# A decoder layer on one core: a shared scratch pool, parameters spread over the dense products, two scan sets ahead of the attention's end, paired sample values, later feed-forward row scales and four result buffers

## The chip, the core and the metric

The kernel runs on 1 core of a Trainium2 chip. TensorE (PE in the profile) multiplies matrices, VectorE (DVE), ScalarE (ACT) and GpSimd (POOL) do the elementwise work, and SyncE (SP) mostly issues transfers. The metric is the device time of one execution in microseconds (us).

## The reference

One layer of a hybrid decoder serves a prompt of 1024 tokens and 8 sample sequences of 4 tokens, 1056 tokens in all, of width 1024, in float32. Each sublayer normalizes its input and adds its result to the stream x:

```
proj = rms_norm(x) @ w_in                         # u (512), q, k, v (512 each)
ssm  = s5(u)            # per channel group: Bu, diagonal complex scan over time, C h + D u, GLU
o    = diff_attention(q, k, v)                    # 4 heads, two softmax maps each, causal
x    = x + concat(ssm, o) @ w_out
x    = x + cross_attention(rms_norm(x), memory)   # 4 heads, 256 memory tokens, ca_wq, ca_wo
h    = rms_norm(x)
x    = x + (silu(conv3(h @ ffn_wg)) * (h @ ffn_wv)) @ ffn_wd   # hidden width 2816
```

The samples attend to 512 cached positions (a paged cache, gathered by a page table) and to cached memory keys and values of their own. The scan starts from zero for the prompt and from a given state for the samples. Keys, values, scan states, the last convolution rows and the memory's keys and values are results too.

## The kernel before, in words

**Products.** A float32 product is done as three products of split operands: `split` (L165) makes a high part on ScalarE and the low rest on VectorE, and `mm3` (L186 to L189) multiplies high by high (L187), high by low (L188) and low by high (L189). Activations lie transposed, channels on partitions and tokens along the free axis, in `Xh` and `Xl`; weights come in blocks of 128 columns as `raw` and are split into `whi` and `wlo`. Tokens are cut into nine tiles (`TILES`: eight of 128 and one of 32) and three column blocks (`TB`: 384, 384 and 288). VectorE and ScalarE calls go through a wrapper, so that all of them carry the line L56; tiles tell them apart.

**Order of the work.** The first part of the layer is written as generators that issue a piece of work and yield a cost estimate. `par` and `drive` (L78, L104) always advance the generator whose sum of costs, divided by a given total, is lowest; a third number in a stream's entry is the share at which it starts, and `until` holds a stream until a name stands in `done`. So the totals `R`, the offsets `S` and the yields set the order in which instructions are written, and with it their place in each engine's queue. The call of `drive` (L1499) runs ten streams: the dense products (`dense_all`, L850), the scan's parameters (`params`), the prompt's attention (`attention_all`), the opening of pools, the scan's table loads, scan sets and outputs (`ssm_tables`, `ssm_datas`, `ssm_outs`, L1090 to L1115), the memory's keys and values, the samples' attention and the samples' scan state.

**Parameters.** `ssm_params` (L330 to L445) computes the discretized scan parameters in scratch that a small allocator (`Carve`, L194) cuts out of four tiles named `scr`. These lie in the tags qT, kT, vt and s3 of the pool `hdB` (L457, L491), which head 1's projections use later, so `dense_all` holds head 1 until `params` is done (L852). Its eight steps yield 100 each. `ssm_setup` (L936 to L992) then builds four tables per quarter in the pool `tb` (L456), among them products `kp` (L967), and stores them to DRAM.

**Heads.** `dense_head` projects q, k and v of one head; `attention` (L680 to L738) computes scores in the two buffers of `ps_s` (tag S), turns the softmax weights `P` and multiplies by values. `open_right` (L900) opens pools when all dense products are done, and `open_left` (L910) opens others when the attention is closed, adding 'left' to `done`.

**Scan sets.** The 512 scan channels are handled in four sets. `ssm_data(q)` (L1009 to L1047) loads the set's inputs `Ug` by SP's queue, waits for 'left', multiplies them into `wp` (L1021), rotates the result by VectorE (`va`, `vb`, `vr`, `vi`), runs eight scans of 128 steps and rotates back into `Hr` and `Hi`. `ssm_out(q)` (L1049) multiplies the states out and turns the result `yt` back (`tp_`, L1087).

**Output gate and w_out.** In the pool block `p4`, `gate(d, b, ...)` (L1569) does one 128-row block of the GLU gate (`zp`) for column block b. At b == 1, `turn_samples` (L1355) transposes the second half of the samples' attention result (`os_` into `po`, L1356), and the mixed rows go to DRAM, from where `load_part` (L1540) loads them for column block b. `update_x` (L1512) adds a product to x and adds its squares to `sqa` (on GpSimd, L1527); `token_rstd` (L1529) sums `sqa` over channels (`sp`, L1534) and computes the tokens' scales `r2`.

**Cross-attention.** The samples' values are 16 groups of four products (`Op`, L1893) in `sample_values` (L1878 to L1917), each with a tile `vt` of 512 KB that GpSimd's queue loads (L1884) into three buffers. They run beside the output projection `ca_wo` (`wo_stage`, L1921), whose parts for the last column block wait for them. `token_rstd` is called at the end (L1955).

**Feed-forward.** `R3`, the scales broadcast over partitions, is made by nine products and nine VectorE copies (L1974 to L1979). For each of 22 hidden blocks `up(m)` (L2001) does three gate blocks (`pg`), scales them by `R3`, does three value blocks (`pv`), then convolution and silu; after each pair of hidden blocks `down` (L2061) multiplies by `ffn_wd` and adds to `xacc`. `xacc` itself is filled from `Xh + Xl` (L2091). Behind the last pair the results are transposed (`pt`, L2078), copied by ScalarE into `yo` (two buffers) and stored row tile by row tile (L2071 to L2082).

**Stages in the trace.** Dense products and attention of the heads run from the start to about 475 us (dense products to about 372), gates from about 550 to 607, w_out to 717, cross-attention to 912, ca_wo to 1026, the feed-forward from there to 1811, the last results to 1822 us.

## Time and profile before

| | |
|---|---|
| median of 3 runs | 1820.39 us (1814.05 to 1829.77) |
| profiled execution | 1823.91 us, span 1822.0 us |
| TensorE busy | 1713.6 us, 94% of the span |
| VectorE, ScalarE, GpSimd busy | 1088.7, 602.8, 509.3 us |
| mean granted clock of TensorE | 0.961 of full speed |

The profile is of one execution; its span runs from the first to the last instruction, and the execution's own time is 1.9 us longer. Busy time of an engine is the time in which one of its instructions ran. PEld is TensorE's loading of weights, which overlaps its products; a name with a q behind it is the engine's sequencer. In a line of the timeline, `out<-in` are the tiles by the program's names, `128x512` partitions by elements, `xN` the number of instructions run together in the line, and what stands in brackets is the idle time of the engine just before it and what ended it. The granted clock is the share of TensorE's full speed that the chip allowed.

### The profile page before, as it was taken

The page shows a single profiled execution, that of the slowest core. Times are in us where ns is not written, and L with a number is a line of the kernel's source. Part 1 is how long each engine was busy: PE and PEld are TensorE (multiplying, and loading weights), DVE is VectorE, ACT ScalarE, POOL GpSimd, SP SyncE. Part 2 cuts the span into 40 slices and gives each one's busy share as a digit, 9 for nine tenths or more (in the row PEclk, how much of TensorE's full clock was granted, in tenths as well). Part 3 has the DMA queues.
Part 4 walks back from the last instruction along what each step waited for, and adds up shares of the span by engine and source line. Part 5 has one row for each costly group of instructions (what it writes and reads, how often), then busy time and mean ns, then how long its engine had stood idle before and what let it go on. Part 6 is the DMA issues. An engine that isn't in the chain of part 4 may idle for free.

```text
span 1822.0 us, 28691 instructions
## 1 busy us (share of the span) xinstructions
PE 1713.6 (94%) x11121; PEld 1596.7 (88%) x11121; DVE 1088.7 (60%) x2563; ACT 602.8 (33%) x1368; POOL 509.3 (28%) x597
## 2 busy tenths in 40 slices
PE   8679999989797899999899999999999999999998
PEld 7458788767685899999769999999999999999997
DVE  6867635666587586555546654654654565555653
ACT  6535335566355343444433211210210211111112
POOL 4456675130300043000033332322312312322210
PEclk9878999989898999999989999999999999999999
DMA  6512232155785722323272111210211211202202
GB/s 174 217 49 80 89 87 91 40 178 172 213 270 163 263 59 64 102 91 94 84 239 70 39 40 31 70 43 28 58 48 35 58 37 46 59 25 58 58 13 97
DMA packets 151809, 170.02 MB, mean 93 GB/s; under 512 B 9528, under 2 KB 125396, under 8 KB 151675
## 3 DMA queue, kind: packets, MB, share of 16 engines
q1 hardware_dynamic: 129650, 114.04, 20.6%
q0 software_dynamic: 10944, 31.95, 5.8%
q10 hardware_dynamic: 11080, 22.21, 3.3%
q8 instruction: 87, 1.43, 0.3%
q14 instruction: 48, 0.39, 0.1%
HBM read 131.86 MB, written 36.30 MB: 92 GB/s over the span
## 4 chain that ended last, share of the span: by engine, by line
PE 79%; DVE 8%; ACT 4%; DMA 3%; issue 1%; SPq 1%; ACTq 0%; POOL 0%; DVEq 0%; POOLq 0%
PE pp L187 5%; PE pp L188 5%; PE pp L189 5%; PE pv L189 5%; PE pv L187 5%; PE pv L188 5%; PE pd L189 5%; PE pd L188 5%; PE pd L187 5%; PE pg L187 5%; PE pg L188 5%; PE pg L189 4%; PE pj L187 2%; PE S L694 2%; PE pj L189 2%; PE pj L188 2%
## 5 line engine op out<-in xcount | busy, mean ns | idle before, releaser
L56 DVE TENSOR_TENSOR xacc<-xacc,pd 128x384 f32<-128x384 f32 (+1 forms) x264 | 135.1, 518 | 169.9 <-PE pd L189 169.9
L56 ACT CAST whi<-raw 128x1024 fp32r<-128x1024 f32 x74 | 77.4, 1049 | 434.0 <-PE pg L188 332.1
L187 PE MATMUL pv<-Xh,whi 128*128 128x384 f32 (+1 forms) x528 | 172.0, 326 | 0.0
L189 PE MATMUL pv<-Xh,wlo 128*128 128x384 f32 (+1 forms) x528 | 171.7, 326 | 0.0
L188 PE MATMUL pv<-Xl,whi 128*128 128x384 f32 (+1 forms) x528 | 171.6, 325 | 0.0
L187 PE MATMUL pd<-ah,dhi 128*128 128x384 f32 (+1 forms) x528 | 171.2, 325 | 0.1
L187 PE MATMUL pg<-Xh,whi 128*128 128x384 f32 (+1 forms) x528 | 171.2, 324 | 0.0
L189 PE MATMUL pd<-ah,dlo 128*128 128x384 f32 (+1 forms) x528 | 170.9, 324 | 0.0
L188 PE MATMUL pd<-al,dhi 128*128 128x384 f32 (+1 forms) x528 | 170.1, 322 | 0.5 <-DVE al L56 0.5
L188 PE MATMUL pg<-Xl,whi 128*128 128x384 f32 (+1 forms) x528 | 170.6, 323 | 0.0
L189 PE MATMUL pg<-Xh,wlo 128*128 128x384 f32 (+1 forms) x528 | 170.1, 322 | 0.0
L56 DVE TENSOR_TENSOR wlo<-raw,whi 128x1024 fp32r<-128x1024 f32 x74 | 108.8, 1471 | 27.7 <-ACT whi L56 21.5
L799 POOL TENSOR_TENSOR raw<-raw,GT 128x1024 f32<-128x1024 f32 x30 | 69.3, 2311 | 158.8 <-DMA raw<-in_ffn_wg_dram 99.4
L187 PE MATMUL pp<-Mh,whi 128*128 128x384 f32 (+1 forms) x336 | 108.9, 329 | 2.5 <-ACT Mh L56 2.5
L187 PE MATMUL pj<-whi,Xh 128*128 128x384 f32 (+1 forms) x288 | 103.0, 360 | 8.0 <-DVE vt L56 7.5
L188 PE MATMUL pp<-Ml,whi 128*128 128x384 f32 (+1 forms) x336 | 109.6, 328 | 0.0
L189 PE MATMUL pp<-Mh,wlo 128*128 128x384 f32 (+1 forms) x336 | 109.5, 327 | 0.0
L188 PE MATMUL pj<-wlo,Xh 128*128 128x384 f32 (+1 forms) x288 | 100.5, 350 | 6.3 <-DVE wlo L56 6.3
L189 PE MATMUL pj<-whi,Xl 128*128 128x384 f32 (+1 forms) x288 | 100.8, 350 | 0.0
L189 PEld LDWEIGHTS pv<-Xh,wlo 128*128 128x128 f32 x528 | 100.0, 189 | 0.1
L187 PEld LDWEIGHTS pv<-Xh,whi 128*128 128x128 f32 x528 | 100.0, 189 | 0.0
L188 PEld LDWEIGHTS pd<-al,dhi 128*128 128x128 f32 x528 | 99.2, 188 | 0.8 <-DVE al L56 0.8
(788 smaller groups left out, 4508.8 us busy)
## 6 DMA issues: line engine op xcount, KB each, us to landing
raw<-in_ffn_wg_dram SPq DMA_DIRECT2D x22, 512.0 KB, 3.9
raw<-in_ffn_wv_dram SPq DMA_DIRECT2D x22, 512.0 KB, 3.9
raw<-in_ffn_wd_dram SPq DMA_DIRECT2D x22, 512.0 KB, 3.8
pg<-in_cache_k_dram SPq DMA_DIRECT2D x32, 256.0 KB, 3.3
V<-in_cache_v_dram SPq DMA_DIRECT2D x32, 256.0 KB, 4.1
kt<-in_cache_mem_k_dram SPq DMA_DIRECT2D x32, 256.0 KB, 3.0
vt<-in_cache_mem_v_dram POOLq DMA_DIRECT2D x16, 512.0 KB, 5.2
raw<-in_w_in_dram SPq DMA_DIRECT2D x48, 128.0 KB, 3.4
```

The source lines that it names most:

```text
L56: return f(*a, **k)
L187: nc.tensor.matmul(out, lhsT=wh, rhs=xh, start=start, stop=False)
L188: nc.tensor.matmul(out, lhsT=wh, rhs=xl, start=False, stop=False)
L189: nc.tensor.matmul(out, lhsT=wl, rhs=xh, start=False, stop=stop)
L694: nc.tensor.matmul(S[:, i, :w], lhsT=qT[pr, 128 * t:128 * t + 128], rhs=kT[pr, c0:c1], start=True, stop=True, tile_position=(64 * i, 0))
L799: nc.gpsimd.tensor_tensor(out=raw, in0=raw, in1=g.unsqueeze(2).to_broadcast([128, KD, 128]), op=ALU.mult)
```

## The change

- The scan parameters' scratch lies in the table pool `tb`, which is now opened on the right side, in the stack of the scan's parameters, with its own five widths; `hdB` loses its tag s3. Head 1's dense products no longer wait for the parameters. The eight steps of `ssm_params` yield 1000 instead of 100, and the stream's total is 38 instead of 28 (thousand).
- `ssm_data` loads its inputs by GpSimd's queue into a pool of its tables and no longer waits for 'left'. Its products go to `ps_w` if that is open, otherwise to a score buffer of the attention; `va`, `vb`, `vr`, `vi` and `H` lie in `tb`. The wait for 'left' stands in `ssm_outs` instead.
- `turn_samples(1, ...)` and the store behind it are issued after the gates of b == 2 instead of b == 1.
- Sample values go two groups at a time, with the next two loads issued after both.
- `token_rstd` for the feed-forward moves into `up(0)`, behind the three value blocks, which come first for m == 0. Then come two gate blocks, the broadcasts of the scales (three times three products, each copied at once by ScalarE), the two gate blocks' scaling and the third gate block.
- `yo` has four buffers (tags hg, hg, th, cv_), and in the last column block VectorE copies every second half.

```diff
-        def __init__(self, tiles):
-            self.room, self.tags = [[t, 0] for t in tiles], {}
+        def __init__(self, tiles, widths):
+            self.room, self.tags = [[t, 0, w] for t, w in zip(tiles, widths)], {}
 
         def tile(self, shape, dtype, name=None, tag=None):
             n = math.prod(shape[1:])
             if tag not in self.tags:
-                r = next(r for r in self.room if r[1] + n <= SEQ)
+                r = next(r for r in self.room if r[1] + n <= r[2])
...
+    tb = pool(ssm, "tb", 1, side="right")
+    TBW = {"CL": 1152, "ST": 1032, "M": 1024, "q1": 576, "q2": 576}
...
-        yield 100
+        yield PY
...
-    tb = pool(p2, "tb", 1)
...
-    st = Carve([hdB.tile([128, SEQ], F32, tag=t, name="scr") for t in ("qT", "kT", "vt", "s3")])
+    st = Carve([tb.tile([128, n], F32, tag=t, name="scr") for t, n in TBW.items()], list(TBW.values()))
...
-    GS, PS = 2, 0.03
+    GS, PS, PY = 2, 0.03, 1000
...
         yield from dense_head(0, first)
-        yield from until(lambda: 'params' in done)
         yield from dense_head(1)
...
-        Ug = (sqs[1], sd)[q % 2].tile([128, 8, 128], F32, tag="Ug", name="Ug")
-        nc.sync.dma_start(out=Ug, in_=u_p[q].rearrange("j c g k -> (j c) g k"))
+        Ug = sqs[q % 3].tile([128, 8, 128], F32, tag="Ug", name="Ug")
+        nc.gpsimd.dma_start(out=Ug, in_=u_p[q].rearrange("j c g k -> (j c) g k"))
         yield 2500
-        yield from until(lambda: 'left' in done)
-        wp = ps_w.tile([128, 2, 4, 128], F32, tag="w", name="wp")
+        wp = (ps_w.tile([128, 2, 4, 128], F32, tag="w", name="wp") if 'left' in done
+              else ps_s.tile([128, 2, 4, 128], F32, tag="S", name="wp"))
         for r in range(4):
...
-        va = sd.tile([128, 4, 128], F32, tag="va", name="va")
-        vb = sd.tile([128, 4, 128], F32, tag="vb", name="vb")
-        vr = sd.tile([128, 4, 128], F32, tag="vr", name="vr")
-        vi = sd.tile([128, 4, 128], F32, tag="vi", name="vi")
+        va = tb.tile([128, 4, 128], F32, tag="q1", name="va")
+        vb = tb.tile([128, 4, 128], F32, tag="q2", name="vb")
+        vv = tb.tile([128, 2, 4, 128], F32, tag="M", name="vv")
+        vr, vi = vv[:, 0], vv[:, 1]
         tt(out=va, in0=wp[:, 0], in1=Rr, op=ALU.mult)
...
-        Hr = sd.tile([128, 4, 129], F32, tag="Hr", name="Hr", bufs=2)
-        Hi = sd.tile([128, 4, 129], F32, tag="Hi", name="Hi", bufs=2)
-        nc.vector.memset(Hr[:, :, 0:1], 0.0)
-        nc.vector.memset(Hi[:, :, 0:1], 0.0)
+        H = tb.tile([128, 2, 4, 129], F32, tag=("CL", "ST")[q % 2], name="H")
+        Hr, Hi = H[:, 0], H[:, 1]
+        nc.vector.memset(H[:, :, :, 0:1], 0.0)
...
-            yield from until(lambda: q in half)
+            yield from until(lambda: q in half and 'left' in done)
             yield from ssm_out(q)
...
-    R = [195, 28, 90, 35, 70, 12]
+    R = [195, 38, 90, 35, 70, 12]
...
-    def token_rstd(pl, ps, r):
-        sp = ps.tile([128, 9], F32, tag="tp", name="sp")
+    def token_rstd(pl, ps, r, tag="tp"):
+        sp = ps.tile([128, 9], F32, tag=tag, name="sp")
...
-            if b == 1:
+            if b == 2:
                 turn_samples(1, tail['os'], ps.tile([128, 512], F32, tag="pj", name="po"))
...
-            for i, (g, s, c) in enumerate(work):
+            for i in range(0, len(work), 2):
                 with tc.high_priority():
-                    for b4 in QUADS:
-                        nc.tensor.matmul(Op[32 * b4:32 * b4 + 32, 256 * g:256 * g + 256],
-                                         lhsT=PT[:, c, s, 32 * b4:32 * b4 + 32], rhs=vts[i][:, b4],
-                                         start=s == 0 and c == 0, stop=s == 1 and c == 1, tile_position=(0, 32 * b4))
-                if i + 3 < len(work):
-                    vts.append(load(*work[i + 3]))
-                yield 500
+                    for j in (i, i + 1):
+                        g, s, c = work[j]
+                        for b4 in QUADS:
+                            nc.tensor.matmul(Op[32 * b4:32 * b4 + 32, 256 * g:256 * g + 256],
+                                             lhsT=PT[:, c, s, 32 * b4:32 * b4 + 32], rhs=vts[j][:, b4],
+                                             start=s == 0 and c == 0, stop=s == 1 and c == 1,
+                                             tile_position=(0, 32 * b4))
+                for w in work[i + 3:i + 5]:
+                    vts.append(load(*w))
+                yield 1000
...
-        token_rstd(wx, ps_t, r2)
     pcs.close()
-    pcq.close()
...
-        for t, (t0, n) in enumerate(TILES):
-            bp = ps_d.tile([128, 128], F32, tag="d", name="bp")
-            nc.tensor.matmul(bp[:, :n], lhsT=r2[:n, t:t + 1].to_broadcast([n, 128]), rhs=ident[:n, :n],
-                             start=True, stop=True)
-            nc.vector.tensor_copy(R3[:, t0:t0 + n], bp[:, :n])
+
+        def row_scales():
+            for t0, n in TB:
+                bp = ps_d.tile([128, 384], F32, tag="d", name="bp")
+                for t in range(t0 // 128, t0 // 128 + 3):
+                    a, m_ = TILES[t]
+                    nc.tensor.matmul(bp[:, a - t0:a - t0 + m_], lhsT=r2[:m_, t:t + 1].to_broadcast([m_, 128]),
+                                     rhs=ident[:m_, :m_], start=True, stop=True)
+                nc.scalar.copy(R3[:, t0:t0 + n], bp[:, :n])
...
-            for t0, n in TB:
+
+            def gate_in(t0, n):
                 pp = ps_g.tile([128, 384], F32, tag="g", name="pg")
                 for k in range(KD):
                     mm3(pp[:, :n], gh_[:, k], gl_[:, k], Xh[:, k, t0:t0 + n], Xl[:, k, t0:t0 + n],
                         k == 0, k == KD - 1)
+                return pp
+
+            def gate_out(t0, n, pp):
...
+            def values_in():
+                for t0, n in TB:
+                    pp = ps_v.tile([128, 384], F32, tag="v", name="pv")
+                    for k in range(KD):
+                        mm3(pp[:, :n], vh_[:, k], vl_[:, k], Xh[:, k, t0:t0 + n], Xl[:, k, t0:t0 + n],
+                            k == 0, k == KD - 1)
+                    pv.append(pp)
+
+            pv = []
+            if m == 0:
+                values_in()
+                token_rstd(fx, ps_d, r2, "d")
+                pps = [gate_in(*TB[b]) for b in range(2)]
+                row_scales()
+                for b in range(2):
+                    gate_out(*TB[b], pps[b])
+                gate_out(*TB[2], gate_in(*TB[2]))
+            else:
+                for t0, n in TB:
+                    gate_out(t0, n, gate_in(t0, n))
             if m == 0:
                 conv_state()
             nc.gpsimd.tensor_copy(hs_[:, :, 0:2], SC[:, m].rearrange("p (b j) -> p b j", j=2))
-            pv = []
-            for t0, n in TB:
-                pp = ps_v.tile([128, 384], F32, tag="v", name="pv")
-                for k in range(KD):
-                    mm3(pp[:, :n], vh_[:, k], vl_[:, k], Xh[:, k, t0:t0 + n], Xl[:, k, t0:t0 + n],
-                        k == 0, k == KD - 1)
-                pv.append(pp)
+            if m:
+                values_in()
...
-                        yo = fa.tile([128, D], F32, tag="hg", name="yo", bufs=2)
+                        yo = fa.tile([128, D], F32, name="yo", tag=("hg", "hg", "th", "cv_")[t % 4],
+                                     bufs=(2, 2, 1, 1)[t % 4])
...
-                            nc.scalar.copy(yo[:m_, 512 * g:512 * g + 512], pt[:m_])
+                            if g and bi == 2:
+                                nc.vector.tensor_copy(yo[:m_, 512:], pt[:m_])
+                            else:
+                                nc.scalar.copy(yo[:m_, 512 * g:512 * g + 512], pt[:m_])
...
```

## Rows read from the trace of the kernel before

**Rows 1.** The page: busy time, share and instructions of each engine.

```profile
PE 1713.6 (94%) x11121; PEld 1596.7 (88%) x11121; DVE 1088.7 (60%) x2563; ACT 602.8 (33%) x1368; POOL 509.3 (28%) x597
```

**Rows 2.** Stretches: length, busy (instructions) per engine, clock, DMA share, GB/s.

```profile
40.00:130.00 90.00, 64.09 (x299) 46.41 (x298) 67.47 (x290) 41.14 (x135) 45.26 (x77) 0.77 0.37 135
...
370.00:470.00 100.00, 89.18 (x722) 70.19 (x720) 61.07 (x250) 61.03 (x157) 20.49 (x38) 0.90 0.58 176
470.00:607.00 137.00, 110.51 (x1029) 93.28 (x1028) 105.66 (x267) 69.77 (x132) 15.56 (x29) 0.89 0.70 212
...
912.00:967.00 55.00, 51.41 (x325) 37.81 (x326) 24.88 (x51) 15.64 (x39) 17.02 (x21) 0.91 0.64 207
...
1036.00:1046.00 10.00, 7.52 (x29) 7.25 (x28) 8.35 (x17) 0.78 (x2) 2.31 (x2) 0.66 0.43 116
1046.00:1811.00 765.00, 764.36 (x4781) 762.22 (x4780) 429.88 (x578) 119.68 (x122) 194.51 (x194) 1.00 0.15 45
1811.00:1822.00 11.00, 4.87 (x37) 3.53 (x35) 0.91 (x2) 4.15 (x8) 0.00 (x0) 0.94 0.53 204
```

**Rows 3.** TensorE's waits, 40 to 130: us in total, times, longest.

```profile
PE pj L188 <- DVE wlo L56: 6.3, 2, 5.9
PE pt L725 <- DVE P L56: 5.1, 2, 3.9
...
PE kp L967 <- ACT Bbi L56: 1.4, 1, 1.4
```

**Rows 4.** The same columns for instructions on scr alone.

```profile
40.00:82.00 42.00, 1.25 (x8) 0.92 (x8) 19.76 (x115) 0.91 (x2) 5.65 (x15) 0.84 0.56 219
82.00:130.00 48.00, 0.00 (x0) 0.00 (x0) 0.00 (x0) 0.00 (x0) 9.94 (x21) 0.72 0.20 62
```

**Rows 5.** Timeline of VectorE: start, us, engine, line, operation, tiles, shape.

```profile
84.27 5.08 DVE L56 TENSOR_TENSOR rs_t<-rsq 128x8 f32<-128x8 f32 x1
...
90.19 0.17 DVE L56 TENSOR_TENSOR rs_t<-rsq 128x8 f32<-128x8 f32 x1
```

**Rows 6.** TensorE's waits, 470 to 607.

```profile
PE tp__6483 L1087 <- DVE yt L56: 7.1, 1, 7.1
PE pt L1398 <- DMA pg<-in_cache_k_dram: 7.0, 2, 6.3
PE po L1356 <- DVE os__5850 L56: 5.4, 1, 5.4
```

**Rows 7.** Timeline of VectorE around scan set 0.

```profile
475.92 0.68 DVE L56 TENSOR_TENSOR va<-wp,Rr 128x512 f32<-128x512 f32 x1
...
480.22 1.36 DVE L56 TENSOR_TENSOR_SCAN vr<-rho,vr 128x128 f32<-128x128 f32 x4
```

**Rows 8.** Timeline of TensorE behind po.

```profile
607.22 0.44 PE L188 MATMUL zp<-Ml,whi 128*128 128x288 f32 x1
...
611.78 0.44 PE L189 MATMUL zp<-Mh,wlo 128*128 128x288 f32 x1
```

**Rows 9.** Tile Op, 905 to 975: duration ns, starts; its engine idle.

```profile
L1893 PE MATMUL Op<-vt,PT x128: 379/403/636, 917.6 to 962.2; 128*32 128x256 f32 x128
...
  issue: 5.7, 16
```

**Rows 10.** Tile vt, 905 to 975: its transfers.

```profile
DMA to landing us min/median/max: 3.9/5.2/7.0
```

**Rows 11.** Timeline of TensorE at the start of the feed-forward.

```profile
1039.24 1.21 PE L1534 MATMUL sp<-ones,sqa 128*128 128x1 f32 x6 [2.48 <-POOL sqa L1527]
```

**Rows 12.** Timeline of VectorE at the start of the feed-forward.

```profile
1026.50 10.50 DVE L56 TENSOR_TENSOR xacc<-Xh,Xl 128x1056 f32<-128x1056 f32 x6
```

**Rows 13.** Timeline of ScalarE at the end.

```profile
1816.16 1.07 ACT L56 COPY yo<-pt 128x512 f32<-128x512 f32 x2 [1.42 <-DMA out_dram<-yo]
...
1818.78 0.34 ACTq L56 DMA_DIRECT2D out_dram<-yo  x1
```

**Rows 14.** Timeline of TensorE: scan set 0's first products.

```profile
461.96 1.09 PE L1021 MATMUL wp<-Ug,ST 128*64 128x128 f32 x12
```

More of the change, by code (lines that the diff above doesn't have):

```diff
@@ L348, in ssm_params @@
             dq(out=braw[:, i], in_=A[n][0].rearrange("(r g) p c -> (g p) r c", g=2))
-        yield 100
+        yield PY
         pp = tp("pp")
@@ L356, in ssm_params @@
         exp_acc(st, dt_, prm[:, 2], 16)
-        yield 100
+        yield PY
         zz = st.tile([128, 16], F32, name="zz")
@@ L361, in ssm_params @@
         exp_acc(st, mag, zz, 16)
-        yield 100
+        yield PY
         ang = st.tile([128, 16, 8], F32, name="ang")
@@ L370, in ssm_params @@
         sincos(st, fl(sn), fl(cs), fl(ang), 128)
-        yield 100
+        yield PY
         nc.vector.memset(Lr[:, :, 0:1], 1.0)
@@ L387, in ssm_params @@
             tt(out=rho, in0=rho, in1=rho, op=ALU.mult)
-        yield 100
+        yield PY
         big = fl(st.tile([128, 8, 128], F32, tag="big", name="big"))
@@ L405, in ssm_params @@
                      ee1[:, :, :w], ee2[:, :, :w])
-        yield 100
+        yield PY
         nre = st.tile([128, 16], F32, name="nre")
@@ L424, in ssm_params @@
         tt(out=fim, in0=fim, in1=den, op=ALU.mult)
-        yield 100
+        yield PY
         par = st.tile([128, 2, 2], F32, name="par")
```

## The prediction, made before the changed kernel was run

> **What bounds the kernel now.** Read first the busy shares: TensorE is busy for 94% of the span [rows 1], so time can come back only where it stands still or runs on the low clock. The windows by stage then say where that is [rows 2]: from 1046 to 1811 us it is busy for 764.36 of 765 us at full clock, and nothing in that stretch of the feed-forward can be won without removing products. Elsewhere, busy time times granted clock falls short of the stretch: 40 to 130 us gives 64.09 x 0.77 = 49 of 90 (41 missing), 370 to 470 gives 80 of 100 (20 missing), 470 to 607 gives 98 of 137 (39 missing), 912 to 967 gives 47 of 55 (8), 1036 to 1046 gives 5 of 10 (5), and 1811 to 1822 has 4.87 of 11. These products are estimates (the clock is averaged over idle time too), but they bound what each edit can return. Third, the waits of TensorE name what it stood for in the first and the third of these stretches [rows 3, 6]; single instructions come last. The sum is made against the profiled execution's own 1823.9 us (span 1822.0 and 1.9 around it), which lies 3.5 above the median of the runs shown and inside their spread of 16 us. A measurement of this kernel can tell about 1% from no change.
>
> **The parameters.** The change removes no instruction here. It moves the scratch from the buffers of head 1 to the scan's own pool, drops the wait of head 1 for the parameters, and spaces eight of their steps by 1000 instead of 100, so that they lie along the nine token tiles of head 0 and into head 1. Before, their vector work stands at 40 to 82 us (19.76 us on VectorE), and 15.59 us on GpSimd lies in 40 to 130 [rows 4]. What waits there: products of head 1 for a low weight half, 5.9 at a time; transposes of head 0's attention for P, 3.9; the table products kp for Bbi, 1.4 [rows 3]. The first is a lock rather than a queue: a 128x8 multiply took 5.08 us, the same form 0.17 us six microseconds later [rows 5], while GpSimd multiplied parameters. If all three went and with them a comparable loss of clock, some 11 + 10 = 21 us return. If the moved GpSimd work locks one more multiply on the path, it is 5 lost. I take 8 gained: the P wait and half of the rest, since kp and the GpSimd chain come back inside head 1, where dense products lie beside them. If those are not there when kp waits, nothing is gained.
>
> The Trainium skill (GPSIMD Engine Reference, 1. Specifications) says that GpSimd and VectorE share SBUF interfaces, and that a VectorE instruction with two SBUF inputs contends for them. The trace agrees with 5.08 against 0.17 us [rows 5]. By this rule spreading frees nothing, as every moved GpSimd microsecond meets another two-input multiply; that is the fourth rival below.
>
> **Two early scan sets.** One set is twelve 128x512 operations of about 0.69 us, two groups of four scans of 1.36 us [rows 7], small copies: 11 us of VectorE. All four sets now run after the attention is closed, in the stretch 470 to 607, where VectorE is busy 105.66 of 137 us and TensorE waits 7.1 us for yt, the last link of a set's chain [rows 2, 6]. After, set 0 and the products of set 1 run beside head 3's attention, where VectorE is busy 61.07 of 100 us [rows 2]: some 20 us leave the crowded stretch. Taken from the path: the 7.1 and about 2 of low clock behind it, 9 in all. At the other end, the 39 missing less 7.6 for the sample wait (next) and 7.0 for cache pages [rows 6] leave some 20 more at most. What is late next is that page wait, a DMA wait that the change leaves. The loads of the samples' inputs move from SP's queue to GpSimd's, four issues in all; there they stand behind the table loads and their waits, and nothing on TensorE stands behind them but their own set. The early products take one of the two score buffers of the attention, from their start until VectorE's last read; queued behind are scores and values of head 3, and behind these the closing of attention and the remaining sets. For set 0 in the trace the first read came at 475.92 and the scans behind the reads began at 480.22 [rows 7], some 4 us; with memory-key products on TensorE to fill this I charge nothing, and leave the price to the third rival.
>
> **The second half of the sample results.** Its transpose po waits 5.4 us for VectorE [rows 6], standing ahead of the four gate blocks of the last column block, which need nothing from it. Behind it 20 products ran 0.24 us apart [rows 8], half of which is clock: 20 x 0.12 = 2.4. Placed after these 48 products (48 x 0.12 = 6 us) po finds its input ready: 7 gained, with 5 and 8 as ends. The store of the rows and the loads of the last block then start 6 us later; two w_out blocks stand ahead of their first use.
>
> **Paired values.** Sixteen groups of sample-value products each cost a switch of the array's shape: 5.7 us of idle over 16 [rows 9], so eight fewer return 2.8. Against that, a pair now needs two buffers of three, and of its own two tiles the second is asked for only when the pair before has ended. Groups went from 917.6 to 962.2 us in 15 steps, 2.97 each [rows 9], 5.9 for two. A pair takes about 1.2 (products), 0.75 (issue) and a landing of 3.9 to 5.2 us [rows 10]: 5.8 to 7.1. Over seven steps that is 1 gained to 8 lost, and the dense blocks beside it end just when the groups do, so no cover is left. I take 2 lost, nearer the short landing because fewer loads are in flight.
>
> The Trainium skill (DMA: Bandwidth & Descriptors, Anatomy of one DMA) fits such a load at 2.0 us and its bytes over 436 GB/s: 3.2 us here, an estimate. By it a pair takes 5.1 and the edit gains its 2.8. The trace differs, with 5.2 at the median [rows 10], and the sum goes by the trace.
>
> **Feed-forward scales.** The column sums sp waited for sqa and took 1.21 us at the head of the queue, after 2.48 us of idle [rows 11]. They move behind the value products. But the value weights' low halves were late as well, behind six adds of 10.50 us on VectorE [rows 12] that the change leaves: at least the 1.21 goes, at most it, the idle and as much again for the clock, 6. Where TensorE's order puts values ahead of gates, the first pair of gate blocks no longer covers the weights' path, and 8 is lost. I take 2.5 gained.
>
> **Four result buffers.** At the end a copy waits 1.42 us for a store to leave its buffer, and the last store is issued at 1818.78 [rows 13]. With two more buffers and every second copy on VectorE, six copies of 0.6 us become three beside three: 1.42 plus 1.8 is 3, and with the earlier such waits 3.5 (ends 2 and 4.5). The stores' own landing stays.
>
> **Sum.** 1823.9 - 8 - 9 - 7 + 2 - 2.5 - 3.5 = 1795.9 us; forecast 1796.
>
> **The rivals.**
> First: only the waits that an edit names directly go. The vector work of parameters and sets is shifted but TensorE stands still as long for other reasons (the page loads, VectorE at 105.66 of 137): 1823.9 - 7 + 2 - 2.5 - 3.5 = 1813. For it: the stretches 40 to 130 and 470 to 607 have several waits of like size, so removing one may expose the next. Against it: the largest of them are what the edits move.
> Second: both stretches give back all that the bounds allow: 1823.9 - 21 - 20 - 7 + 2 - 2.5 - 3.5 = 1772. For it: 41 and 39 us are missing there. Against it: page waits and half-clock restarts remain.
> Third, the slower one: the early sets hold a score buffer. Place: head 3's attention. If the set's reads queue behind other VectorE work while scores wait for the buffer, each of two sets delays the close of attention by its hold; in the trace of before products of set 0 began at 461.96 [rows 14] and were read until 480.2 [rows 7], 18 us while nobody needed the buffer. At 16 per set the early start returns nothing: 1795.9 + 9 + 32 = 1837, slower than before. It decides from a hold of some 14 us per set on, where it eats all that the other parts gain. Against it: TensorE has other work in that stretch, and VectorE is free 39% of the time.
> Fourth: GpSimd's moved parameter work locks VectorE elsewhere: the 8 gained become 5 lost, 1809.
>
> **How the numbers follow.** Forecast 0.50, first 0.20, second 0.13, third 0.10, fourth 0.07. The forecast's own range is 1784 to 1808 from the ends of its middling terms. The limits of 1% around the median are 1802 and 1839. Faster by over 1%: 0.85 of the forecast, the second whole, a tenth of the first, 0.58. Slower by over 1%: half of the third, 0.05. Within 1%: 0.37. The range reaches from just above the second rival to between the first and the third, 1774 to 1822, and leaves out the third whole and the ends of the second.
>
> **What would show it.** Right: no wait of po for os_ of several us; no copy of the results waiting for a store; the wait for yt gone and set 0's scans at 400 to 460 us; no multiply of 5 us near 84 us; head 1's first products without a 6 us wait; the stage's end moved from 607 to about 583. Wrong: the last value group of the samples later than 962 relative to the stage's start by more than 5; scores of head 3 waiting for va or vb; TensorE idle just after the last ca_wo product; a new multiply of several us between 100 and 200 us. If the stretch 40 to 130 still lasts 90 for the same work, the first term is wrong.

## The result, and the profile after

The changed kernel takes 1840.03 us (median of 4 runs, 1839.26 to 1845.19) against 1820.49 us of the kernel before in the same comparison. The ratio is 1.0114, with a 95% interval of 1.0090 to 1.0139: some 20 us slower, where 1796 us and a range of 1774 to 1822 had been forecast. The profiled execution took 1840.73 us, with a span of 1838.8.

The windows by stage of the changed kernel, cut at the same points of the work as [rows 2] (columns as there; the gates follow by themselves):

```profile
40.00:130.00 90.00, 73.19 (x360) 55.92 (x359) 72.82 (x307) 45.02 (x157) 40.33 (x73) 0.91 0.37 136
...
370.00:470.00 100.00, 86.94 (x731) 67.58 (x729) 69.72 (x266) 61.01 (x150) 22.24 (x42) 0.91 0.63 200
...
930.00:985.00 55.00, 50.96 (x328) 37.50 (x326) 24.89 (x53) 15.83 (x41) 17.01 (x21) 0.94 0.64 207
...
1054.00:1064.00 10.00, 7.17 (x29) 6.75 (x28) 8.20 (x17) 0.78 (x2) 2.60 (x4) 0.66 0.45 117
1064.00:1829.00 765.00, 764.36 (x4781) 762.51 (x4780) 429.65 (x570) 120.53 (x125) 197.21 (x192) 1.00 0.15 45
1829.00:1839.00 10.00, 4.65 (x36) 3.42 (x34) 2.92 (x5) 2.60 (x5) 0.00 (x0) 0.97 0.59 225
```

[rows 2] and the list of stages end the gates of the kernel before at 607 us; its last gate product starts at 615.6, at 632.5 after the change. From 470 us to the first product of w_out, before and after:

```profile
470.00:615.70 145.70, 119.21 (x1076) 101.98 (x1075) 109.89 (x277) 73.31 (x139) 16.33 (x30) 0.88 0.72 220
470.00:632.80 162.80, 132.59 (x1052) 105.91 (x1052) 93.27 (x239) 67.84 (x128) 15.47 (x29) 0.89 0.67 218
```

This stretch is 17 us longer. VectorE did do less there, 93.27 instead of 109.89 us, as the sets' move should have it, and TensorE did about as many instructions (1052 instead of 1076), yet was busy for 132.59 instead of 119.21 us. Everything behind it lasts as long as before, only later. The first stretch holds more work than before (73.19 instead of 64.09 us busy), and that lead is gone by 370 us. Starts of a few products, each from the view of its tile (us):

| | before | after |
|---|---|---|
| first product of u (dense part behind head 1) | 176.5 | 151.3 |
| last dense product of the heads | 371.9 | 369.6 |
| last transpose of P (attention's end) | 456.3 | 460.0 |
| first product of set 0 | 462.0 | 412.9 |
| last output product of the sets (yp) | 573.1 | 570.8 |
| last value product of the samples' pages | 592.2 | 595.1 |
| first gate product | 574.9 | 600.8 |
| first product of w_out | 615.7 | 632.8 |
| first product of the feed-forward | 1027.1 | 1044.9 |
| last product of the feed-forward | 1811.6 | 1829.4 |

The loss appears at one place, between the sets' last output product and the first gate product. Before, the gate started 1.8 us behind that product, and now 30 us behind it. The sets end 2 us earlier and the gates, once started, take 9 us less (31.7 instead of 40.7), so 17 of the 28 us are left at w_out. The waits of TensorE from 470 to 640 us of the changed kernel (us in total, times, longest):

```profile
PE Op L1452 <- DMA V<-in_cache_v_dram: 9.0, 4, 4.6
PE yp L1058 <- ACT yt L56: 4.3, 1, 4.3
PE zp L187 <- ACT th L56: 3.9, 1, 3.9
PE zp L187 <- ACT Mh L56: 2.8, 1, 2.8
```

The wait of po for `os_`, 5.4 us in [rows 6], is gone. The wait of `tp_` for `yt` is down from 7.1 to 1.5 us, while one of `yp` for `yt`, 4.3, is new. The samples' value pages come first now. The timeline says how the gate hangs on them:

```profile
594.18 1.94 PE L1452 MATMUL Op<-V,aT 128*32 128x512 f32 x8 [3.16 <-DMA V<-in_cache_v_dram]
...
596.05 1.93 PE L1452 MATMUL Op<-vs__82,aT 32*32 32x512 f32 x8
...
598.04 0.35 DVE L56 TENSOR_SCALAR os__6004<-Op,hmask 128x128 f32<-128x128 f32 x1 [12.55 <-PE Op L1452]
...
599.59 0.31 ACT L56 ACTIVATE oj<-os__6004 128x128 f32<-128x128 f32 x1 [14.88 <-DVE os__6004 L56]
...
599.89 2.29 ACT L56 CAST Mh<-gT 128x768 fp32r<-128x768 f32 x3
...
600.76 1.01 PE L187 MATMUL zp<-Mh,whi 128*128 128x384 f32 x2 [2.79 <-ACT Mh L56]
```

The gate's operands `Mh` are cast from `gT`, whose part for these three casts was complete at 577 us, and have nothing to do with the pages. ScalarE nevertheless stood for 14.88 us and cast them only behind the samples' result `oj`. Before, the casts stood in ScalarE's queue ahead of that result (its timeline in the kernel before):

```profile
569.35 1.58 ACT L56 CAST Mh<-gT 128x768 fp32r<-128x768 f32 x2
...
598.98 0.31 ACT L56 ACTIVATE oj<-os__5850 128x128 f32<-128x128 f32 x1
```

The page loads and the last page product are what the third cast waits for in the built program, and no data of theirs goes into it: it is the memory.

### The profile page after: what moved, and what is told of

Read it like the earlier page. It is cut to its first block, busy times and chain, and to the rows that moved or that the text cites. A ratio compares the mean times of both kernels' runs of the same rounds, so it can differ in the third digit from the quotient of the medians.

```text
span 1838.8 us, 28652 instructions
## 1 busy us (share of the span) xinstructions
PE 1724.2 (94%) x11121; PEld 1598.2 (87%) x11121; DVE 1087.2 (59%) x2553; ACT 602.1 (33%) x1368; POOL 512.1 (28%) x601
## 4 chain that ended last, share of the span: by engine, by line
PE 79%; DVE 8%; DMA 4%; ACT 3%; issue 1%; POOL 1%; SPq 0%; ACTq 0%; DVEq 0%
PE pp L187 5%; PE pp L188 5%; PE pp L189 5%; PE pv L189 5%; PE pv L187 5%; PE pv L188 5%; PE pd L188 5%; PE pd L189 5%; PE pd L187 5%; PE pg L187 5%; PE pg L188 4%; PE pg L189 4%; PE pj L187 2%; PE S L695 1%; PE pj L189 1%; PE pj L188 1%
## 5 line engine op out<-in xcount | busy, mean ns | idle before, releaser
L187 PEld LDWEIGHTS pd<-ah,dhi 128*128 128x128 f32 x528 | 99.2, 188 | 0.9 <-ACT ah L56 0.5
```

Source lines behind the costliest of these rows:

```text
L187: nc.tensor.matmul(out, lhsT=wh, rhs=xh, start=start, stop=False)
```

## The experiments

Two things hold for all of them. The kernel before ran beside each, with medians of 1817.9 to 1820.5 us. And a single profile has a spread of its own: the changed kernel and pool_order have the same order of products on TensorE up to pool_order's first gate product, yet their last transposes of P stand at 460.0 and 465.5 us. So stages are compared by their length or over several traces, and times by the medians.

**Where the pools lie.** `tb` used to lie low, among the buffers that are given up with the attention. On the right side, where pools are stacked downwards, it takes 18,400 bytes per partition, and every pool opened there later moves down (`sqA` is also 4,096 bytes wider, since `Ug` now lies in it). These are the places in the built programs (bytes per partition, from and to):

```
          before            after             pool_order
wx        106912 116304     106912 116304     106912 116304   gate: work tiles
mpB        81568 106912      81568 106912      81568 106912   gate: operands Mh, Ml
sa        124192 148784     101696 126288     122688 147280   samples' attention: pages V
ptb       148800 156768     126304 134272     147296 155264   samples' attention: tables
sqA       156768 173664     134272 155264     101696 122688   scan tables, sets 0 and 3
```

In the changed kernel `sa` covers the end of the gate's operands and all of its work tiles. pool_order opens the three pools in another order, and nothing else:

```diff
-        sqs.append(pool(pk, "sqA", 1, side="right"))
         ptb = pool(pk, "ptb", 1, side="right")
         sa = pool(pk, "sa", 1, side="right")
+        sqs.append(pool(pk, "sqA", 1, side="right"))
```

> The changed kernel with two pools of the samples' attention (its tables and its pages) opened ahead of the scan's table pool, so that they lie above the memory of the gate's operands; nothing else differs. Theory A (in the changed kernel the operands of the gate lie in the memory of the samples' value pages, so the gate waits for the last page): the first gate product starts at 572 to 580 us instead of 600.8, the first product of w_out at 607 to 616 instead of 632.8, and the time is 1814 to 1824 us. Theory B (the early scan sets push the samples' attention and the gate back by VectorE and queue order; memory has no part): the gate still starts at 595 or later and the time stays at 1836 to 1843 us.

Measured: 1833.80 us, ratio 1.0087 (1.0068 to 1.0107), 6 less than the changed kernel. The casts stand ahead of `oj` again; the gate starts 13.5 us behind the last yp instead of 30, and w_out starts at 623.1 instead of 632.8. The direction is theory A's, but not the size: the gate starts at 592.4 us, short of both theories, the time falls by less than half of what theory A said, and the two intervals overlap. In this trace w_out stood 7.0 us for reloaded rows, and the attention ended 5.5 us later than in the changed kernel; how much either took was not shown. So the memory was tried alone, without the other parts. layout_only keeps only the moved pool with what it needs (the sets' tiles in `tb`, inputs by GpSimd's queue, no wait of head 1):

```diff
-    GS, PS, PY = 2, 0.03, 1000
+    GS, PS, PY = 2, 0.03, 100
...
-    R = [195, 38, 90, 35, 70, 12]
+    R = [195, 28, 90, 35, 70, 12]
...
         yield 2500
+        yield from until(lambda: 'left' in done)
...
-            if b == 2:
+            if b == 1:
...
```

(and the old text of sample values, scales and result buffers).

> The changed kernel with all else undone but the pool's move: steps of 100, the wait of the scan sets for the attention's end, the second half of the sample results at b == 1, single sample values, the scales at the end of the output projection, two result buffers. Theory A: the gate starts behind the last page, at 592 us or later, where the kernel before started at 574.9, and the time is 1830 to 1845 us. Theory B: the gate starts at 570 to 580 us and the time is 1812 to 1824 us, as before.

Measured: 1831.52 us, ratio 1.0075 (1.0060 to 1.0089); the gate starts at 592.2 us, behind the last page product at 586.5, and ScalarE stands for the samples' result as in the changed kernel:

```profile
591.04 0.31 ACT L56 ACTIVATE oj<-os__5847 128x128 f32<-128x128 f32 x1 [18.22 <-DVE os__5847 L56]
...
591.34 3.28 ACT L56 CAST Mh<-gT 128x768 fp32r<-128x768 f32 x6
```

This is theory A. order_clean is layout_only with pool_order's line:

> layout_only (pool moved, all other parts undone) with the two pools of the samples' attention opened ahead of the scan's table pool; one changed line beside layout_only. Theory A (gate operands in the memory of the samples' pages): the gate starts at 572 to 580 us instead of 592.2 and the time is 1814 to 1822 us against 1831.5 of layout_only, the same as before. If the 12 us of layout_only have another cause (the scan's inputs by GpSimd's queue, its rotation in the table pool), the time stays at 1828 to 1834 us.

Measured: 1818.42 us, ratio 0.9991 (0.9969 to 1.0013). The gate starts at 573.5 us, while the last page product comes at 589.6 (TensorE, then ScalarE):

```profile
573.53 0.69 PE L187 MATMUL zp<-Mh,whi 128*128 128x384 f32 x1
```

```profile
566.22 3.30 ACT L56 CAST Mh<-gT 128x768 fp32r<-128x768 f32 x6
```

The intervals of the two don't touch, and one line lies between them, the order of three pools. So their place costs 13 us when it stands alone, and the two traces show how: with `sa` over the gate's operands, the gate waits for the pages.

**The early sets.** order_late_sets gives pool_order's sets their wait for 'left' back.

> pool_order with all four scan sets waiting for the attention's end again. By the prediction's term the early sets are worth 9 us: 1840 to 1845 us, and the stretch from the last transpose of P to the first w_out product grows from 157.6 by 9. If the early start is worth nothing, because the samples' attention and not the sets ends that stretch, the time stays at 1828 to 1836 us and the stretch grows by 0 to 4.

Measured: 1824.84 us, ratio 1.0040 (1.0020 to 1.0059): the early sets are not worth 9 us, they cost 9. Neither expectation had that. The stretch from the last transpose of P to w_out is even shorter without them, 152.1 against 157.6 us, and the attention ends earlier. The first suspect was the prediction's third rival, the hold of the score buffer; early_copy shortens it:

```diff
+        if 'left' not in done:
+            ww = tb.tile([128, 2, 4, 128], F32, tag="ST", name="ww")
+            nc.scalar.copy(ww, wp)
+            wp = ww
```

> pool_order with one addition: while the attention is open, ScalarE copies a set's products out of the score buffer into the table pool at once, and VectorE reads the copy. If the hold of the score buffer (products of set 0 from 415.8, last read at 424.3) delays the attention, its last transpose of P comes back from 465.5 to 456 to 460 us, and the time falls to 1824 to 1830 us. If VectorE's work for the sets in that stretch or the late page loads delay it, the last transpose stays at 461 to 466 and the time at 1830 to 1837 us.

Measured: 1822.96 us, ratio 1.0013 (0.9991 to 1.0034), 11 less than pool_order. But the reason given for it fell: the attention's last transpose of P stayed at 464.8 us. What had gone is seen on TensorE's timeline. In the changed kernel, output products of a set (yp) and score products of the samples (Sp) alternate two by two:

```profile
478.12 0.41 PE L1403 MATMUL Sp<-KT,Qb 128*32 128x128 f32 x2
478.46 0.48 PE L1064 MATMUL yp<-CL,H 64*128 64x128 f32 x2
478.88 0.41 PE L1403 MATMUL Sp<-KT,Qb 128*32 128x128 f32 x2
479.21 0.48 PE L1064 MATMUL yp<-CL,H 64*128 64x128 f32 x2
479.63 0.41 PE L1403 MATMUL Sp<-KT,Qb 128*32 128x128 f32 x2
479.96 0.48 PE L1064 MATMUL yp<-CL,H 64*128 64x128 f32 x2
```

Both groups are issued with raised priority, and the scheduler mixed them. There are 50 such changes in the changed kernel and in pool_order (34 with yp products of 64*128 as here, 16 with those of 128*128), 4 in order_late_sets, and none in the kernel before or in early_copy. after_yp_plain and yp_plain take the raised priority from yp alone (the line is replaced by one without effect), in the changed kernel and in pool_order; one change is left.

```diff
-        with tc.high_priority():
+        if True:
```

> The changed kernel with one thing different: the products of a scan set's output (yp) are issued without raised priority, so that on TensorE they no longer alternate two by two with the samples' score products (Sp), 50 changes of shape between the two that took 20.0 us in the changed kernel's trace, where the same products in whole blocks take some 6. Theory C (the alternation is the price of the early sets): 50 changes become 1 or 2, and as the gates still wait for the samples' last page, which itself comes earlier, the time falls by 6 to 14 to 1826 to 1834 us. Theory D (the sets' own work in the attention's stretch is the price): the time stays at 1837 to 1842 us.

Measured: 1833.94 us, ratio 1.0086 (1.0063 to 1.0109), against 1840.03: 6 less. The two intervals overlap, but the slowest of its six runs (1838.89) is below the fastest of the changed kernel's four (1839.26).

> pool_order and the same plain priority. Theory C: pool_order's 1833.8 falls by 8 to 13 to 1821 to 1826 us, as early_copy did, whose copy had removed the alternation too. Theory D: 1830 to 1837 us.

Measured: 1826.92 us, ratio 1.0049 (1.0031 to 1.0067), against 1833.80: 7 less, just short of what theory C said, and the intervals do not touch (1.0067 and 1.0068). The blocks in yp_plain's timeline of TensorE:

```profile
478.02 1.08 PE L1403 MATMUL Sp<-KT,Qb 128*32 128x128 f32 x32
...
541.01 2.06 PE L1064 MATMUL yp<-CL,H 64*128 64x128 f32 x32
```

Two Sp take 0.07 us here and two yp 0.13, 0.20 together; alternating, such a pair took 0.76 (478.12 to 478.88); the granted clock was 1.00 in all three places. At 0.56 each, 25 pairs lose up to 14 us of TensorE's time, an estimate, and its busy time up to w_out is 13 us longer than before; 6 to 7 show in the whole. The Trainium skill (TensorEngine Tiling (Array Packing), Key Properties) says that changing the tiling mode drains TensorE. This trace agrees: 0.28 us for each change here; in [rows 9], where groups of 128*32 stand between products of 128*128, TensorE idles 0.36 us ahead of each group.

So most of the 9 us that order_late_sets won back is the alternation: yp_plain, with the early sets and one change, is at 1.0049 and order_late_sets, without them and with four, at 1.0040, with intervals that overlap. What stays of the early sets: in all ten traces with them the last transpose of P lies at 460.0 to 465.5 us, in all eight without them at 453.7 to 458.2. That is work moved ahead of the attention's end. Which of its pieces delays the end was not taken apart.

**The second half of the sample results.** ends_only puts four parts on the kernel before: this move, the paired values, the scales and the result buffers. po_only has the move alone, tail_only the other three.

```diff
-            if b == 1:
+            if b == 2:
                 turn_samples(1, tail['os'], ps.tile([128, 512], F32, tag="pj", name="po"))
```

> The kernel before with four of the six parts alone: the second half of the sample results at b == 2, paired sample values, the later scales, four result buffers; memory and scan as before. The prediction's terms: 7 gained, 2 lost, 2.5 and 3.5 gained, so about 11 us faster than before, 1805 to 1810 us. The rival: the moved transpose lets the reload of the last column block come late, w_out waits about 6 us for it, values and scales move nothing and the buffers give 1: 1813 to 1822 us, no difference from before.

Measured: 1823.83 us, ratio 1.0026 (1.0011 to 1.0042), slower than either expectation.

> The kernel before with the second half of the sample results at b == 2, nothing else. The prediction: 7 faster, 1811 to 1813 us. The rival from ends_only: the gates end about 13 us earlier, w_out then stands 8 to 9 us for the reloaded rows and its clock falls, so that the time is between no change and 5 us slower, 1818 to 1825 us.

Measured: 1822.36 us, ratio 1.0011 (0.9992 to 1.0030). The gates do end earlier (last gate product at 605.7 instead of 615.6 us), and then w_out stands. Waits of TensorE from 455 to 640 us in po_only:

```profile
PE pp L187 <- ACT Mh L56: 9.2, 1, 9.2
PE tp__6483 L1087 <- DVE yt L56: 7.5, 1, 7.5
```

> The kernel before with paired sample values, later scales and four result buffers alone. The prediction: 2 lost, 2.5 and 3.5 gained, 1814 to 1816 us. The stage times of the changed kernel (values 44.2 us against 44.6, feed-forward 784.5 against 784.5, end 9.4 against 10.4) say 1 us gained: 1816 to 1820 us.

Measured: 1819.35 us, ratio 0.9993 (0.9973 to 1.0013). The sum of the two is below what ends_only took, but inside the intervals; whether the four have a price together was not settled. order_b1 and plain_b1 take the move back from pool_order and from yp_plain:

> The changed kernel with the two pools reordered (pool_order) and the second half of the sample results back at b == 1. In pool_order w_out waited 7.0 us for the reloaded rows. If that wait is the price of the move, it goes, and a wait of 4 to 8 us for the transpose comes back ahead of the last gate blocks: 1828 to 1838 us, the same as pool_order within 4. By the prediction's term (7 gained by the move) this kernel is 7 slower than pool_order: 1840 us.

> yp_plain with the second half of the sample results back at b == 1. po_only cost 0 to 4 on the kernel before, so 0 to 4 faster than yp_plain: 1818 to 1824 us.

Measured: 1833.18 us, ratio 1.0086 (1.0061 to 1.0111), and 1826.36 us, ratio 1.0056 (1.0034 to 1.0077). Against 1833.80 and 1826.92 neither shows a difference; the second lies 2 us above what was expected. In po_only the wait of po, 5.4 us in [rows 6], is traded for 9.2 us of w_out. In these two pairs w_out stands for its rows either way: 5.2 us in order_b1 and 6.0 in plain_b1, with the transpose back at b == 1, and 7.0 and 4.6 in pool_order and yp_plain.

**The spread of the parameters.**

```diff
-    GS, PS, PY = 2, 0.03, 1000
+    GS, PS, PY = 2, 0.03, 100
...
-    R = [195, 38, 90, 35, 70, 12]
+    R = [195, 28, 90, 35, 70, 12]
```

> pool_order with the parameters' steps at 100 and their total at 28 again (the scratch stays in the table pool, and head 1 waits for nothing). By the prediction's term the spread is worth up to 8 us: 1838 to 1843 us. If the stalls only move to later, since TensorE's busy time up to 370 us was 323.7 before and 323.6 after, the time stays at 1828 to 1837 us, and the last dense product of the heads ends at 368 to 373 us.

Measured: 1828.83 us, ratio 1.0065 (1.0041 to 1.0089), 5 less than pool_order, with intervals that overlap; here the alternation, too, was less (41 changes). So it was repeated where there is none.

> plain_b1 with the parameters' steps at 100 and their total at 28. If the spread is worth nothing by itself, the same as plain_b1 within 3 us; if order_py100's 5 us against pool_order were the spread's own price, 4 to 6 faster than plain_b1, 1813 to 1819 us, and so perhaps faster than the kernel before.

Measured: 1821.54 us, ratio 1.0012 (0.9996 to 1.0028), again 5 less than plain_b1, and here the intervals are apart. In kernels with the early sets the spread costs about 5 us. The last dense product of the heads lies at 369.6 to 373.3 us in eight traces with steps of 1000, and at 368.3 to 370.7 in six with 100 and no wait of head 1. The means are 2.5 us apart, so about half of the price is paid by then; where the rest is paid was not found.

**Everything mended.** all_mended is plain_b1_py100 with early_copy's copy; clean_plus_tail is order_clean with the three late parts.

> plain_b1_py100 with early_copy's copy of the sets' products out of the score buffer: the early sets, with the pool order, the plain priority, the transpose at b == 1 and the steps at 100. If the copy is worth something beside the alternation that it happened to remove (early_copy 1823.0 against yp_plain 1826.9), 1815 to 1819 us, the same as before or a little faster; if not, 1820 to 1823 as plain_b1_py100.

Measured: 1817.65 us, ratio 0.9992 (0.9980 to 1.0004).

> order_clean with the three late parts added (paired values, later scales, four result buffers): all sets behind the attention, steps of 100, the transpose at b == 1. order_clean and tail_only were both the same as before within 0.1%: 1814 to 1820 us, the same as before.

Measured: 1820.42 us, ratio 0.9998 (0.9982 to 1.0014). Both are the same as the kernel before, and so is order_clean. The two differ by the early sets with their two remedies, so the early sets without side costs are worth nothing that can be measured. No version was found that is measurably faster.

The way down from the changed kernel, one edit a line:

| kernel | median us | ratio (95%) |
|---|---|---|
| changed kernel | 1840.03 | 1.0114 (1.0090 to 1.0139) |
| + pools in another order | 1833.80 | 1.0087 (1.0068 to 1.0107) |
| + yp at plain priority | 1826.92 | 1.0049 (1.0031 to 1.0067) |
| + transpose back at b == 1 | 1826.36 | 1.0056 (1.0034 to 1.0077) |
| + steps of 100 | 1821.54 | 1.0012 (0.9996 to 1.0028) |
| + products copied out of the score buffer | 1817.65 | 0.9992 (0.9980 to 1.0004) |

6, 7, 1, 5 and 4 make 22: the loss of 20, and 2 that lie within the intervals around the kernel before. Only at the second and the fourth step do the intervals not touch, and each is backed by a second pair; the first step rests on layout_only and order_clean, and the third and the last are within their intervals.

## Why the prediction was wrong, step by step

**The step that failed first is one that the prediction did not price:** "It moves the scratch from the buffers of head 1 to the scan's own pool". It was costed as a move of vector work. As a move of memory it pushed the samples' pages under the gate's operands and made the gate wait for them: 13 us when it stands alone, 6 when it is undone in the changed kernel (within its intervals). No rival had it. The diff shows it (a pool moves to the right side, ahead of others), and the profile of the kernel before can't: there the two don't touch.

**The parameters, 8 gained: wrong in sign.** The wait of head 1 for its low weight half did fall, from 5.9 to 0.6 us at its longest, and the dense part reached u 25 us earlier. But the spread costs 5 us. The 5.08 us multiply of [rows 5] is gone, and a tiny operation of head 1 stands instead (timelines of VectorE and GpSimd in the changed kernel):

```profile
91.35 4.08 DVE L56 SCALAR_TENSOR_TENSOR rsq<-rs_t,rsq 32x4 f32<-32x4 f32 x1
```

```profile
91.67 3.74 POOL L800 TENSOR_TENSOR raw<-raw,G 128x1024 f32<-128x1024 f32 x2
```

What GpSimd multiplies beside it are weights, not parameters. And with steps of 100 the same operation takes longer (VectorE in plain_b1_py100):

```profile
93.19 5.22 DVE L56 SCALAR_TENSOR_TENSOR rsq<-rs_t,rsq 32x4 f32<-32x4 f32 x1
```

So it is not the price of the spread, and that the fourth rival's "5 lost" has the right size is luck. The step that failed is "kp and the GpSimd chain come back inside head 1, where dense products lie beside them". Head 1's last product starts at 150.7 us, and the long wait of kp ends at 173.8. Waits of TensorE from 130 to 370 us in the changed kernel:

```profile
PE bc L774 <- DVE y L56: 6.0, 1, 6.0
PE kp L967 <- DVE ksT L56: 4.8, 1, 4.8
PE kp L967 <- POOL CLt L954: 3.3, 1, 3.3
```

The longest there before was 4.0. pool_order and plain_b1, with steps of 1000, have these waits too (the last one 2.1 us in plain_b1); in order_py100 and plain_b1_py100, with steps of 100, kp does not wait there, and bc 0.4 us. So the cover of dense products that was thought to be there for kp was not. As other waits stand with steps of 100 (4.0 us of scores for mx), that these make up the 5 us was not shown.

**The two early sets, 9 gained: wrong in sign.** The premises held: set 0's scans run at 421 to 425 us, the wait of `tp_` for `yt` fell from 7.1 to 1.5, and VectorE was relieved by 17 us where it was crowded. But VectorE did not end that stretch. In the changed kernel the samples' pages did, and the prediction had named page waits as late next without letting them eat the gain; without the side costs, too, the relief brought nothing (all_mended against clean_plus_tail). The price was on TensorE, where the order of two raised groups changed: 6 to 7 us. The third rival was the right part of the kernel with the wrong mechanism. Its hold of a score buffer is short (products from 415.8, scans from 424.3 us in pool_order), and taking it away left the attention's end where it was. That the rival's 1837 us lies near the measured 1840 is luck. Two of the sums there are off as well: 39 less 7.6 and 7.0 is 24, of which 15 are left beside the 9; and by the rival's own sum, which also takes back the 9, a hold of 9.5 us per set is enough to eat all gains, not 14.

**The second half of the sample results, 7 gained: nothing.** The wait of po went as forecast. What failed is "two w_out blocks stand ahead of their first use": they don't cover the store, the reload and the split, and w_out stood 9.2 us in po_only.

**Paired values, 2 lost: nothing, or 0.4 gained.** The tile's view in the changed kernel:

```profile
L1894 PE MATMUL Op<-vt,PT x128: 379/403/636, 935.8 to 980.0; 128*32 128x256 f32 x128
...
  issue: 5.1, 16
```

The groups take 44.2 us instead of 44.6, and the idle time at changes of shape is 5.1 instead of 5.7 us in 16, not halved, because no pair was formed. In TensorE's queue the sixteen groups still stand one by one with dense products between them:

```profile
947.11 0.64 PE L1894 MATMUL Op<-vt,PT 128*32 128x256 f32 x8
...
948.14 0.34 PE L188 MATMUL pp<-Ml,whi 128*128 128x384 f32 x1
...
949.11 0.64 PE L1894 MATMUL Op<-vt,PT 128*32 128x256 f32 x8
```

So the step "eight fewer" failed: no switch was saved, and the price of a pair was not tried either. The loads landed in 5.3 us at the median, and TensorE waited 0.7 us for them in all.

**Scales, 2.5 gained: nothing.** First and last feed-forward products are 784.5 us apart in both. The first twelve sums go early, as before, and behind them two waits of 1.34 and 1.49 us stand where one of 2.48 stood in [rows 11] (timeline of TensorE):

```profile
1055.92 0.76 PE L1533 MATMUL sp<-ones,sqa 128*128 128x1 f32 x6 [1.34 <-POOL sqa L1526]
1058.17 0.69 PE L189 MATMUL pv<-Xh,wlo 128*128 128x384 f32 x1 [1.49 <-DVE wlo L56]
```

The low halves wait for the same adds as in [rows 12], which the prediction had named:

```profile
1045.52 8.16 DVE L56 TENSOR_TENSOR xacc<-Xh,Xl 128x1056 f32<-128x1056 f32 x4
```

**Four result buffers, 3.5 gained: 1.** The mechanism is right. No copy waits for a store any more (ScalarE's timeline), and the last store follows its last product as before:

```profile
1832.48 0.59 ACT L56 COPY yo<-pt 128x512 f32<-128x512 f32 x1 [0.75 <-PE pt L2103]
...
1833.92 0.57 ACT L56 COPY yo<-pt 32x512 f32<-32x512 f32 x1 [0.86 <-PE pt L2103]
1834.32 1.77 ACTq L56 DMA_DIRECT2D out_dram<-yo  x2
```

From the last feed-forward product to the end it is 9.4 instead of 10.4 us. Of the 3.5, the 1.8 for shorter copies and the earlier waits did not show.

**The chances.** Slower by over 1% had 0.05. The missing time of the stretches 40 to 130 and 470 to 607 was read as time to be won back, with waits named for less than half of it. That the edits might add waits of a new kind there was put into one rival alone.

## What to carry to other kernels

Read a moved pool as a moved neighbour: list from where to where every pool opened after it lies, and ask which later buffer now lies on one that ends late, since the wait that this makes stands at an instruction that the edit doesn't touch. When work is moved so that two groups with raised priority become ready together, look at the order that the scheduler makes of them on TensorE: small products of two shapes, alternating, can cost as much as the wait that the move removes (6 to 7 us here, against 7.1). And time that is missing in a stretch bounds a gain only until the next link is named; where that link is a transfer that the edit leaves, the gain is nothing until an experiment says otherwise.

## What the runs showed of the hardware that was not expected

A change between the shapes 128*32 and 64*128 on TensorE took some 0.28 us beyond the products themselves (0.76 us for a pair that takes 0.20 in blocks). The 50 changes of the changed kernel, 16 of them between 128*32 and 128*128, were worth 6 to 7 us of the kernel in two pairs, in one of which the intervals overlap. And relieving VectorE in its most crowded stretch brought nothing that can be measured: from 470 us to w_out it is busy for 97.61 us in all_mended, with the early sets, and for 109.64 in clean_plus_tail, without them, and the two kernels are at 0.9992 (0.9980 to 1.0004) and 0.9998 (0.9982 to 1.0014) of the kernel before.
